# A two-layer mixture-of-experts decoder on one core: shared expert blocks summed by twos, the block order moved, smaller DMA sums, x adds on GpSimd

## The chip, the cores and the metric

The kernel runs on one core of one Trainium2 chip. The metric is the device time of one execution in microseconds (us). Three executions of the kernel before took 2149.96, 2151.9 and 2156.48 us; their median, 2151.9 us, is the time before.

## The reference

Two layers work on x of 512 tokens by 1024 numbers, in float32. Each has a mixer (layer 0: block attention and gated linear attention; layer 1: a gated delta net) and then a mixture of experts (MoE), both closed by a layer norm of `alpha * x + gate * f(...)`. The change lies almost wholly in the MoE:

```python
scores = sigmoid(xf @ router_w)                # 512 x 64 experts
topi   = top 6 of the experts in the 4 best of 8 groups, by scores + bias
topw   = scores[topi] / sum * ROUTED_SCALE
for e in range(64):                            # the tokens that chose e
    routed[tok] += w * ((silu(xf[tok] @ w_gate[e]) * (xf[tok] @ w_up[e])) @ w_down[e])
shared = (silu(xf @ sh_gate) * (xf @ sh_up)) @ sh_down
return routed + shared
```

`w_gate` and `w_up` are 1024 x 256, `w_down` is 256 x 1024: 3 MB of weights per expert, 64 experts, two layers. A layer has 3072 pairs of token and expert.

## The kernel before

The core sorts the experts by their number of tokens (all but the first two) and puts them in 38 blocks of 128 rows per layer: 20 **singles** (one expert each, places 0 to 19 of the sorted list), 14 **twos** (two experts, 64 rows each) and 4 **fours** (32 rows each). `blocks()` builds the table `BLOCKS`; `share()` tells experts with more tokens than their rows to leave the rest to an extra stage that runs only where it is needed.

`moe()` (from L1480 on) goes over the blocks in one loop. For each block there is, on TensorE (PE):

- the **turn** (L1324): 8 transposes of the gathered rows of x;
- **widen** (L1336): the gate and up projections, 16 matmuls;
- the **turn back** (L1347): 2 transposes of the hidden rows;
- **narrow** (L1369): the down projection. A four has 4 weights of 1 MB, and its narrow falls in two halves, each with two of them (the generator yields between).

One turn of the loop issues narrow of block b-1 and widen of block b, the turn of b+1, the turn back of b, and the one-hot matmuls (L1270) that say which tokens block b+2 or b+3 gathers. PE's order is exactly the order in which the Python code issues it (`manual_schedule`); the other engines are ordered by a scheduler.

How the result gets into x differs. A **single** is multiplied on VectorE (DVE, L1375) and added to an array `acc` in DRAM by an indirect DMA of 128 rows that accumulates (L1376, issued by GpSimd, POOL). After the last block, `acc` is read back in 8 pieces (L1615) and added to x by 8 DVE additions (L1616). A **shared** block (two or four) is split into a high and a low part (`yh`, `yl`; L1383 to L1385) and summed by PE with one-hot matrices (**combine**, L1396): for each of 4 token tiles and 2 halves of the columns 2 matmuls fill a bank, and one DVE addition of 128 x 512 (L1397) puts it into x. These 8 rounds per shared block come in two portions of 4: after widen, and after the turn and turn back.

The SP queue loads the weights in order (L1302): gate and up of expert e (2 MB), then down of expert e-3 (1 MB). Gate and up have 5 buffers, down has a ring of 3 (`slot`, L202): a load of down waits until narrow has read the third one before it, a load of gate and up until widen has read the fifth one before it. Whatever stands behind in SP's order waits too.

At the end of layer 0's mixer `out_project` calls `fill`, which works off a queue of small pieces of the modulation of layer 1; its last piece is `mod_end`, 16 transposes (L268) and 4 reductions (L269).

Of the kernel before, what the change touches and what calls it, by code (L numbers as in the profile page):

```python
# [18 lines left out]
P = 128  # L19
# [29 lines left out]

def blocks():  # L50


    def shared(k, n, m):
        w = P // m
        return [tuple((k + (g if j % 2 == 0 else -1 - g) + n * ((j + 1) // 2) // (m // 2), w * j, w)
                      for j in range(m)) for g in range(n // m)]

    def spread(out, more, at0=0.5, end=0):

        n = len(out) + len(more)  # L60
        at = {int((k + at0) * (n - end) / len(more)) for k in range(len(more))}
        a, b = iter(out), iter(more)
        return [next(b if k in at else a) for k in range(n)]

    alone = [((k, 0, P),) for k in range(ALONE)]
    twos = shared(ALONE, TWOS, 2)
    fours = shared(ALONE + TWOS, E - ALONE - TWOS, 4)
    return alone[:SINGLE] + spread(spread(twos, fours), alone[SINGLE:], 0, 1)
# [65 lines left out]
class Kernel:  # L134
# [1032 lines left out]
    def share(self, M):  # L1167
# [4 lines left out]
        runs, k = [], ALONE  # L1172
# [154 lines left out]
    def widen(self, M, G):  # L1327
# [4 lines left out]
        h = G["h"] = M["pool"].tile([P, FE], F32, tag="hh", name="hh", bufs=2)  # L1332
# [18 lines left out]
    def narrow(self, M, G):  # L1351

        nc, hT, pool = self.nc, G["hT"], M["pool"]
        one = G.get("one")
        if one:
            (yh,) = [pool.tile([P, D], FR, tag="yh", name="yh", bufs=2)]
# [14 lines left out]
        if one:  # L1371
            yf = yh.bitcast(F32)
            for h, py in enumerate(pys):
                cs = slice(512 * h, 512 * h + 512)
                nc.vector.tensor_mul(yf[:, cs], py, M["grow"][:, cs])  # L1375
            nc.gpsimd.indirect_dma_start(out=M["acc"], out_offset=bass.IndirectOffsetOnAxis(ap=G["tok"], axis=0),  # L1376
                                         in_=yf, in_offset=None, bounds_check=S + P - 1, compute_op=OP.add)
# [93 lines left out]
    def moe(self, l, hT, nxt, pre=None):  # L1471
# [32 lines left out]
        def loads():  # L1504

            last = []
            for k, b in enumerate(BLOCKS):
# [4 lines left out]
                W.append([(a, n, x) for (_, a, n), x in zip(b, w)])  # L1512
# [40 lines left out]
        with ExitStack() as es:  # L1553
            M["pool"] = self.pool(f"exp{l}", ctx=es)
            todo, units = [], []
# [11 lines left out]
            with self.tc.manual_schedule(engines={mybir.EngineType.PE}):  # L1567
                fetch(sum(2 * len(x) for x in BLOCKS[:LEAD]) + 2)
                self.turn(M, G[0])
                for b in range(NB + 1):  # L1570
# [3 lines left out]
                    if b > 0:  # L1574
                        row.append(self.narrow(M, G[b - 1]))
                        if not G[b - 1]["one"]:
                            todo.append(G[b - 1])
                    if b < NB:
                        fetch(sum(2 * len(x) for x in BLOCKS[:b + LEAD]) + 2)
                        G[b]["w"], G[b]["one"] = W[b], len(W[b]) == 1  # L1580
                        row.append(self.widen(M, G[b]))
                    if not todo:
                        row.reverse()
                    for x in row:
                        next(x)
                    for x in row:
                        for _ in x:
                            pass
                    if todo and b < NB:
                        units = [lambda g=todo, t=t, h=h: self.combine(g, t, h) for t in range(TT) for h in range(2)]  # L1590
                        todo = []
                    for u in units[:4]:
# [3 lines left out]
                    if b < NB and not units:  # L1596
# [3 lines left out]
                    if b < NB and units:  # L1600
# [4 lines left out]
                    units = []  # L1605
# [168 lines left out]
    def run(self):  # L1774
# [5 lines left out]
        with ExitStack() as es:  # L1780
# [8 lines left out]
            def fill(n=3):  # L1789

                n, left[0] = n + left[0], 0
                for i in range(n):
# [5 lines left out]
                    if i and len(queue) == 1:  # L1798
# [12 lines left out]
            self.out_project(mixed, d["ev_w_out"][0], grow, d["x"][0], fill, (0, 1, 4, 5, 6, 7, 2, 3))  # L1811
# [86 lines left out]
```

## Time and profile before

| | |
|---|---|
| median of 3 executions | 2151.9 us |
| profiled execution | 2150.13 us |
| its span in the trace | 2148.1 us |
| mean granted TensorE clock | 0.967 |
| PE busy | 1955.6 us, 91% |
| weight loads of PE (PEld) | 1193.5 us, 56% |
| VectorE busy | 1236.2 us, 58% |
| ScalarE (ACT) busy | 508.3 us, 24% |
| GpSimd busy | 441.2 us, 21% |
| DMA moved | 572.18 MB, mean 266 GB/s |

The span runs from the first to the last instruction of the profiled execution. The expert loop of layer 0 lies at about 402 to 1028 us, that of layer 1 at about 1491 to 2117 us. A granted clock of 1 is 2.4 GHz, 0.5 is 1.2 GHz. The idle time of an engine is put down to what ended it ("releaser").

### The profile page before, as it was taken

How to read it: one execution, taken by the hardware profiler on the slowest of the kernel's cores; microseconds unless marked ns; L12 is line 12 of the kernel's file. 1: busy time of each engine (PE TensorE's matmuls, PEld its weight loads, DVE VectorE, ACT ScalarE, POOL GpSimd, SP SyncE). 2: the span in 40 equal slices, each digit the busy share in tenths (PEclk: the TensorE clock that was granted, in tenths of full speed). 3: DMA queues.
4: the chain of work that ended last, by engine and by line, in shares of the span. 5: the costliest groups of instructions: out<-in, count | busy, mean ns of one | idle time of the engine just before them, and what ended most of it. 6: DMA issues, size and time to landing. Idle time of an engine off the chain costs nothing. (4 is left out here: it accounts for less than half of the span.)

```text
span 2148.1 us, 28655 instructions
## 1 busy us (share of the span) xinstructions
PE 1955.6 (91%) x10619; PEld 1193.5 (56%) x10619; DVE 1236.2 (58%) x3169; ACT 508.3 (24%) x969; POOL 441.2 (21%) x313
## 2 busy tenths in 40 slices
PE   4999878999999999999688999999999999998995
PEld 3777778644443443443567877888443444443432
DVE  6666687844444553542778778578453535544436
ACT  3412533111111111111334455523111111111110
POOL 1222234111010110101034445144211010110102
PEclk9999998999999999999899999999999999999997
DMA  7765455998998989988332111128989989989893
GB/s 296 257 240 186 182 199 195 352 330 325 406 349 351 389 316 361 381 325 300 96 118 59 40 60 60 46 99 309 357 335 365 363 327 402 353 317 405 329 348 126
DMA packets 128679, 572.18 MB, mean 266 GB/s; under 512 B 16943, under 2 KB 54255, under 8 KB 72473
## 3 DMA queue, kind: packets, MB, share of 16 engines
q1 hardware_dynamic: 103600, 499.81, 60.1%
q0 software_dynamic: 19632, 55.79, 9.3%
q10 hardware_dynamic: 5304, 14.72, 1.9%
q8 instruction: 85, 1.39, 0.3%
q14 instruction: 58, 0.47, 0.1%
HBM read 550.33 MB, written 34.61 MB: 272 GB/s over the span
## 5 line engine op out<-in xcount | busy, mean ns | idle before, releaser
L1336 PE MATMUL ps_mm<-wslot,xT 128*64 128x512 f32 (+2 forms) x1216 | 404.5, 596 | 1.1 <-ACT xT L1325 0.8
L1369 PE MATMUL ps_mm<-wslot,hT 128*64 128x512 f32 (+2 forms) x1024 | 329.6, 627 | 20.1 <-DMA wslot<-in_moe_w_down_dram 19.9
L1338 DVE SCALAR_TENSOR_TENSOR hh<-hh,t,ps_mm 128x256 f32<-128x256 f32 x76 | 36.5, 480 | 434.5 <-ACT hh L1337 434.5
L1336 PE MATMUL ps_mm<-parts,xT 128*64 128x512 f32 (+2 forms) x832 | 280.0, 595 | 0.7 <-ACT xT L1325 0.4
L1336 PEld LDWEIGHTS ps_mm<-wslot,xT 128*64 128x64 f32 (+2 forms) x1216 | 142.1, 148 | 218.9 <-issue 205.7
L1369 PEld LDWEIGHTS ps_mm<-wslot,hT 128*64 128x64 f32 (+2 forms) x1024 | 105.5, 152 | 225.1 <-issue 197.5
L232 PE MATMUL ps_mm<-parts,hTh 128*128 128x256 f32 x704 | 206.7, 295 | 14.0 <-DVE op L400 6.9
L1294 POOL DMA_INDIRECT xg<-hd,idx x76 | 86.3, 1136 | 615.1 <-PE ps_tr L1396 525.4
L233 PE MATMUL ps_mm<-parts,hTh 128*128 128x256 f32 x704 | 204.0, 291 | 4.9 <-DVE parts L220 4.2
L234 PE MATMUL ps_mm<-parts,hTl 128*128 128x256 f32 x704 | 203.3, 291 | 0.0
L225 POOL TENSOR_TENSOR parts<-wslot,parts 128x512 fp32r<-128x512 f32 (+1 forms) x79 | 140.6, 1807 | 241.9 <-ACT parts L218 241.8
L1397 DVE TENSOR_TENSOR x<-x,ps_tr 128x512 f32<-128x512 f32 x288 | 183.6, 680 | 11.1 <-PE ps_tr L1396 10.4
L1337 ACT ACTIVATE hh<-ps_mm 128x256 f32<-128x256 f32 x76 | 29.2, 384 | 613.7 <-PE ps_mm L1336 613.7
L1376 POOL DMA_INDIRECT acc<-yh,row x40 | 64.8, 1620 | 498.9 <-DVE yh L1375 498.9
L1336 PEld LDWEIGHTS ps_mm<-parts,xT 128*64 128x64 f32 (+2 forms) x832 | 93.7, 144 | 130.5 <-issue 122.9
L1396 PE MATMUL ps_tr<-yh,ohs 128*128 128x512 f32 x288 | 137.4, 477 | 26.1 <-DVEq L1690 14.0
L232 PEld LDWEIGHTS ps_mm<-parts,hTh 128*128 128x128 f32 x704 | 137.3, 195 | 17.7 <-DVE op L400 4.6
L1325 ACT ACTIVATE xT<-ps_tr 128x512 f32<-128x512 f32 x152 | 84.0, 597 | 245.0 <-PE ps_tr L1324 245.0
L233 PEld LDWEIGHTS ps_mm<-parts,hTh 128*128 128x128 f32 x704 | 137.4, 195 | 6.8 <-DVE parts L220 4.8
L234 PEld LDWEIGHTS ps_mm<-parts,hTl 128*128 128x128 f32 x704 | 136.8, 195 | 2.2 <-issue 0.9
L234 PE MATMUL ps_mm<-hTh,parts 128*128 128x512 f32 (+1 forms) x296 | 120.6, 407 | 9.1 <-POOL parts L225 9.1
L232 PE MATMUL ps_mm<-hTh,parts 128*128 128x512 f32 (+1 forms) x296 | 123.7, 418 | 5.1 <-ACT parts L218 2.5
(456 smaller groups left out, 3124.3 us busy)
## 6 DMA issues: line engine op xcount, KB each, us to landing
wslot<-in_moe_w_down_dram SPq DMA_DIRECT2D x128, 1024.0 KB, 10.4
wslot<-in_moe_w_gate_dram SPq DMA_DIRECT2D x76, 1024.0 KB, 8.2
wslot<-in_moe_w_up_dram SPq DMA_DIRECT2D x76, 1024.0 KB, 11.7
parts<-in_moe_w_gate_dram SPq DMA_DIRECT2D x52, 1024.0 KB, 10.3
parts<-in_moe_w_up_dram SPq DMA_DIRECT2D x52, 1024.0 KB, 8.8
wslot<-in_ada_w_dram SPq DMA_DIRECT2D x44, 1024.0 KB, 5.6
wslot<-in_od_w_in_dram SPq DMA_DIRECT2D x16, 1024.0 KB, 6.2
wslot<-in_ev_w_in_dram SPq DMA_DIRECT2D x12, 1024.0 KB, 6.4
```

Of the source, the lines that this page charges most:

```text
L225: eng.tensor_sub(lo[:, ks], v[:, ks], hi[:, ks].bitcast(F32))
L232: self.nc.tensor.matmul(out, ah, bh, start=(i == 0), stop=False)
L233: self.nc.tensor.matmul(out, ah, bl, start=False, stop=False)
L234: self.nc.tensor.matmul(out, al, bh, start=False, stop=(i == n - 1))
L1294: self.nc.gpsimd.indirect_dma_start(out=xg, out_offset=None, in_=M["hd"], in_offset=bass.IndirectOffsetOnAxis(ap=idx, axis=0), bounds_chec ...
L1325: nc.scalar.activation(xT[:, 4 * g:4 * g + 4], pt.rearrange("p (k c) -> p k c", k=4), AF.Copy)
L1336: nc.tensor.matmul(pv[a:a + n], xT[:, i, a:a + n], w[0][:, :, i], start=(i == 0), stop=(i == KT - 1))
L1338: nc.vector.scalar_tensor_tensor(h, h, G["wt"], pg[:, FE:], op0=OP.mult, op1=OP.mult)
L1369: nc.tensor.matmul(py[a:a + n], hT[:, k, a:a + n], w[1][:, k, 512 * h:512 * h + 512], start=(k == 0), stop=(k == 1))
L1376: nc.gpsimd.indirect_dma_start(out=M["acc"], out_offset=bass.IndirectOffsetOnAxis(ap=G["tok"], axis=0), in_=yf, in_offset=None, bounds_che ...
L1396: nc.tensor.matmul(po, G["oh"][:, t], y[:, cs], start=(i + k == 0), stop=(i == len(Gs) - 1 and k == 1))
L1397: nc.vector.tensor_add(self.x[t][:, cs], self.x[t][:, cs], po)
```

## The change

1. **Combine by twos.** Two shared blocks are collected; then 4 matmuls fill a bank before one DVE addition, 8 rounds for two blocks (`full`, `todo`). Only the last two shared blocks of a layer are summed alone. The number of matmuls stays the same; the additions fall from 18 x 8 to 10 x 8 per layer.
2. **Block order.** `spread(..., 0.5, 3)` turns the row of block sizes from `1 1 1 1 2 1 2 1 4 1 2 1 2 1 2 1 4 ...` into `1 1 1 2 1 2 1 4 1 2 1 2 1 1 2 1 4 ...`; the end turns from `... 4 1 2 2` into `... 1 4 2 2`.
3. **Fours.** The second half of a four's narrow is issued after the turn and turn back, not right behind widen; a pair whose second block is a four is summed one turn of the loop later (`late`).
4. **First of a pair.** Where no sum is due, widen of the single is issued ahead of narrow of the two (`row.reverse()`).
5. **DMA sums.** Singles use a buffer of their own (`ys`, one copy) in place of a copy of `yh`; the buffer `hh` has one copy in place of two. The DMA accumulates only the expert's share of rows: 128 for places 0 to 8, 96 for places 9 to 13, 80 for places 14 to 19. That is 5 x 32 + 6 x 48 = 448 rows of 4 KB less per layer. PE still computes 128 rows.
6. **Reading acc back.** 4 DMAs of 512 KB, in the last three turns of the loop, into the buffers of gathered rows, and 4 additions of 128 x 1024 per layer on GpSimd, in place of 8 DMAs of 256 KB and 8 additions on DVE behind the last turn.
7. **fill.** `out_project` of layer 0 calls `fill(3, False)`, so that `mod_end` comes inside its last stage and not behind it.

```diff
+def width(k):
+    return P if k < SINGLE + 7 else 96 if k < SINGLE + 12 else 80
...
-    alone = [((k, 0, P),) for k in range(ALONE)]
+    alone = [((k, 0, width(k)),) for k in range(ALONE)]
...
-    return alone[:SINGLE] + spread(spread(twos, fours), alone[SINGLE:], 0, 1)
+    return alone[:SINGLE] + spread(spread(twos, fours), alone[SINGLE:], 0.5, 3)
...
-        h = G["h"] = M["pool"].tile([P, FE], F32, tag="hh", name="hh", bufs=2)
+        h = G["h"] = M["pool"].tile([P, FE], F32, tag="hh", name="hh", bufs=1)
...
-            (yh,) = [pool.tile([P, D], FR, tag="yh", name="yh", bufs=2)]
+            yf = pool.tile([P, D], F32, tag="ys", name="ys", bufs=1)
...
-            nc.gpsimd.indirect_dma_start(out=M["acc"], out_offset=bass.IndirectOffsetOnAxis(ap=G["tok"], axis=0),
-                                         in_=yf, in_offset=None, bounds_check=S + P - 1, compute_op=OP.add)
+            nc.gpsimd.indirect_dma_start(out=M["acc"], out_offset=bass.IndirectOffsetOnAxis(ap=G["tok"][:one], axis=0),
+                                         in_=yf[:one], in_offset=None, bounds_check=S + P - 1, compute_op=OP.add)
...
-                    if not todo:
+                    four = b > 0 and len(BLOCKS[b - 1]) > 2
+                    full = len(todo) == 2 or (todo and shared > nshared - 2)
+                    if not full and not four:
                         row.reverse()
                     for x in row:
                         next(x)
-                    for x in row:
+                    for x in row[four:]:
                         for _ in x:
                             pass
-                    if todo and b < NB:
-                        units = [lambda g=todo, t=t, h=h: self.combine(g, t, h) for t in range(TT) for h in range(2)]
+                    units, late = late, []
+                    if full and b < NB:
+                        late = [lambda g=todo, t=t, h=h: self.combine(g, t, h) for t in range(TT) for h in range(2)]
                         todo = []
+                        if not four:
+                            units, late = units + late, []
...
-                    if b == NB - 1:
-                        for t in range(TT):
-                            for h in range(2):
-                                cs = slice(512 * h, 512 * h + 512)
-                                y = self.wk("acc")
-                                nc.gpsimd.dma_start(y, M["acc"][t * P:(t + 1) * P, cs])
-                                nc.vector.tensor_add(self.x[t][:, cs], self.x[t][:, cs], y)
+                    if NB - 3 <= b < NB:
+                        for t in back[b][0]:
+                            nc.gpsimd.tensor_add(self.x[t], self.x[t], M["xg"][(NB - 3 + t) % 3])
+                        for t in back[b][1]:
+                            nc.gpsimd.dma_start(M["xg"][(NB - 3 + t) % 3], M["acc"][t * P:(t + 1) * P])
...
+                    for x in row[:four]:
+                        for _ in x:
+                            pass
...
-                    if i and len(queue) == 1:
+                    if wait and i and len(queue) == 1:
                         left[0] = n - i
                         return
...
-            self.out_project(mixed, d["ev_w_out"][0], grow, d["x"][0], fill, (0, 1, 4, 5, 6, 7, 2, 3))
+            self.out_project(mixed, d["ev_w_out"][0], grow, d["x"][0], lambda: fill(3, False), (0, 1, 4, 5, 6, 7, 2, 3))
```

PE's order at a four, before (the first `hT 32x512` row is the first half of its narrow, the `wslot_4117` row widen of the single behind it, `yh` and `yl` rows are combine):

```order
L1440 MATMUL ps_mm<-wd,sh 128x512 x2
L1369 MATMUL ps_mm<-wslot,hT 32x512 x8
L1336 MATMUL ps_mm<-wslot_4117,xT 128x512 x8
L1369 MATMUL ps_mm<-wslot,hT 32x512 x8
L1396 MATMUL ps_tr<-yh,ohs 128x512
...
L1324 MATMUL ps_tr<-call,xg_2911 128x128 x8
L1347 MATMUL ps_sm<-call,hh 128x128 x2
```

The same place now (lines 1334, 1346, 1357, 1379 and 1449 are the old 1324, 1336, 1347, 1369 and 1440):

```order
L1379 MATMUL ps_mm<-wslot,hT 32x512 x8
L1346 MATMUL ps_mm<-parts,xT 128x512 x8
L1334 MATMUL ps_tr<-call,xg_2910 128x128 x8
L1357 MATMUL ps_sm<-call,hh 128x128 x2
...
L1449 MATMUL ps_mm<-wd,sh 128x512 x2
L1379 MATMUL ps_mm<-wslot,hT 32x512 x8
L1346 MATMUL ps_mm<-wslot_4029,xT 64x512
```

The turn, the turn back and a piece of the shared expert (L1449) now stand between widen and the second half, and no combine stands between the second half and widen of the next two (the `64x512` row).

PE's order at the two that follows a four, behind widen of that two and narrow of the single, before:

```order
L1369 MATMUL ps_mm<-wslot,hT 128x512 x4
L1347 MATMUL ps_sm<-call,hh 128x128 x2
L1324 MATMUL ps_tr<-call,xg_2912 128x128 x8
...
L1440 MATMUL ps_mm<-wd,sh 128x512 x2
L1369 MATMUL ps_mm<-wslot,hT 64x512 x8
L1336 MATMUL ps_mm<-parts,xT 128x512 x8
L1396 MATMUL ps_tr<-yh,ohs 128x512
L1396 MATMUL ps_tr<-yl,ohs 128x512
```

Now:

```order
L1379 MATMUL ps_mm<-wslot,hT 128x512 x4
L1357 MATMUL ps_sm<-call,hh 128x128 x2
L1334 MATMUL ps_tr<-call,xg_2911 128x128 x8
...
L1379 MATMUL ps_mm<-wslot,hT 64x512 x8
L1346 MATMUL ps_mm<-wslot_4117,xT 128x512 x8
L1405 MATMUL ps_tr<-yh,ohs 128x512
L1405 MATMUL ps_tr<-yl,ohs 128x512
```

Narrow of the two keeps its place behind the single; behind it, and behind widen of the next single, comes the sum of a pair (L1405), 16 matmuls there and 16 after the turn.

The end of a layer, now (the last four, then the two twos; the second `hT 64x512` row reads a weight from another buffer):

```order
L1346 MATMUL ps_mm<-wslot_16179,xT 64x512
L1334 MATMUL ps_tr<-call,xg_11979 128x128 x8
L1357 MATMUL ps_sm<-call,hh 128x128 x2
L1379 MATMUL ps_mm<-wslot,hT 32x512 x8
L1379 MATMUL ps_mm<-wslot,hT 64x512
L1379 MATMUL ps_mm<-wslot_16270,hT 64x512
```

Narrow of the first of the two twos follows the second half of the four at once; before, a single stood between the last four and these twos.

## Rows read from the trace of the kernel before

**Rows 1.** Page: busy times, DMA queues (packets, MB, share of 16 engines).

```profile
PE 1955.6 (91%) x10619; PEld 1193.5 (56%) x10619; DVE 1236.2 (58%) x3169; ACT 508.3 (24%) x969; POOL 441.2 (21%) x313
...
q0 software_dynamic: 19632, 55.79, 9.3%
```

**Rows 2.** Windows: length; busy PE, PEld, DVE, ACT, POOL; clock, DMA share, GB/s.

```profile
400.00:1000.00 600.00, 577.31 (x2380) 260.29 (x2379) 277.98 (x847) 79.01 (x150) 68.12 (x55) 0.98 0.93 356
500.00:600.00 100.00, 96.57 (x409) 42.88 (x410) 45.18 (x135) 12.11 (x23) 9.94 (x8) 1.00 0.97 376
...
980.00:990.00 10.00, 7.03 (x15) 1.47 (x15) 1.23 (x2) 0.63 (x1) 0.00 (x0) 0.66 1.01 428
```

**Rows 3.** Waits of PE: total us, times, longest us.

```profile
PE ps_mm L1369 <- DMA wslot<-in_moe_w_down_dram: 19.9, 8, 4.2
PE ps_tr L1396 <- DVEq L1690: 14.0, 2, 8.0
...
PE ps_tr L1396 <- DVE yl L1385: 7.8, 9, 1.0
```

**Rows 4.** Timeline of PE, sum of one two: start us, duration us, instruction, [idle].

```profile
579.51 0.80 PE L1396 MATMUL ps_tr<-yh,ohs 128*128 128x512 f32 x1
...
580.38 0.40 PE L1396 MATMUL ps_tr<-yh,ohs 128*128 128x512 f32 x1
580.62 0.39 PE L1396 MATMUL ps_tr<-yl,ohs 128*128 128x512 f32 x1
...
582.26 1.31 PE L1324 MATMUL ps_tr<-call,xg 128*128 128x128 f32 x8
...
583.75 0.48 PE L1396 MATMUL ps_tr<-yh,ohs 128*128 128x512 f32 x1
...
585.89 0.64 PE L1336 MATMUL ps_mm<-parts,xT 128*64 128x512 f32 x1
```

**Rows 5.** Timeline of PE: second half of a four's narrow, first and last four.

```profile
544.88 3.62 PE L1369 MATMUL ps_mm<-wslot,hT 128*32 128x512 f32 x14 [1.40 <-DMA wslot<-in_moe_w_down_dram]
...
982.81 6.61 PE L1369 MATMUL ps_mm<-wslot,hT 128*32 128x512 f32 x14 [3.01 <-DMA wslot<-in_moe_w_down_dram]
```

**Rows 6.** PE and SP behind the first four; landing of that load, of all.

```profile
548.43 0.50 PE L1396 MATMUL ps_tr<-yh,ohs 128*128 128x512 f32 x1
...
555.58 7.09 PE L1336 MATMUL ps_mm<-wslot,xT 128*64 128x512 f32 x32
...
569.36 3.65 PE L1369 MATMUL ps_mm<-wslot,hT 128*64 128x512 f32 x16
...
547.69 0.33 SPq L1302 DMA_DIRECT2D wslot<-in_moe_w_down_dram  x1
...
wslot<-in_moe_w_down_dram SPq DMA_DIRECT2D x1, 1024.0 KB, 13.4
...
DMA to landing us min/median/max: 4.6/10.0/20.6
```

**Rows 7.** Timeline of SP: loads behind narrow of a two.

```profile
573.04 0.33 SPq L1302 DMA_DIRECT2D wslot<-in_moe_w_down_dram  x1
...
581.15 0.33 SPq L1302 DMA_DIRECT2D wslot<-in_moe_w_down_dram  x1
```

**Rows 8.** Timeline at the end of each layer, and a GpSimd operation of 128 x 1024.

```profile
1018.85 0.50 PE L1396 MATMUL ps_tr<-yh,ohs 128*128 128x512 f32 x1
...
1036.01 0.79 PE L1396 MATMUL ps_tr<-yh,ohs 128*128 128x512 f32 x1 [7.98 <-DVEq L1690]
...
2108.36 0.50 PE L1396 MATMUL ps_tr<-yh,ohs 128*128 128x512 f32 x1
...
2123.06 0.79 PE L1396 MATMUL ps_tr<-yh,ohs 128*128 128x512 f32 x1 [6.01 <-DVEq L1690]
...
2129.88 2.38 POOL L330 TENSOR_TENSOR x<-x,wd 128x1024 f32<-128x1024 f32 x1 [1.55 <-ACT x L329]
```

**Rows 9.** Timeline of PE ahead of the MoE of layer 0.

```profile
355.39 1.12 PE L268 MATMUL ps_tr<-call,acc 128*128 128x128 f32 x4 [4.12 <-DVE mod L269]
```

More of the change, by code (lines that the diff above doesn't have):

```diff
@@ L1171, in share @@
         of = {k: (a, n) for b in BLOCKS for k, a, n in b}
-        runs, k = [], ALONE
+        runs, k = [], SINGLE
+        for n in sorted({width(k) for k in range(SINGLE, ALONE)}, reverse=True):
+            m = sum(width(j) == n for j in range(SINGLE, ALONE))
+            if n < P:
+                runs.append((k, k + m))
+            k += m
         for n, m in ((TWOS, 2), (E - ALONE - TWOS, 4)):
@@ L1353, in narrow @@
         nc, hT, pool = self.nc, G["hT"], M["pool"]
-        one = G.get("one")
+        one = G.get("one", 0)
         if one:
-            (yh,) = [pool.tile([P, D], FR, tag="yh", name="yh", bufs=2)]
+            yf = pool.tile([P, D], F32, tag="ys", name="ys", bufs=1)
         elif "y" not in G:
@@ L1371, in narrow @@
         if one:
-            yf = yh.bitcast(F32)
             for h, py in enumerate(pys):
@@ L1511, in loads @@
                 w = [[] for _ in es]
-                W.append([(a, n, x) for (_, a, n), x in zip(b, w)])
+                W.append([(a, n if len(b) > 1 else P, x) for (_, a, n), x in zip(b, w)])
                 for x, e in zip(w, es):
@@ L1554, in moe @@
             M["pool"] = self.pool(f"exp{l}", ctx=es)
-            todo, units = [], []
+            todo, late, shared = [], [], 0
+            nshared = sum(len(b) > 1 for b in BLOCKS)
+            back = {NB - 3: ((), (0, 1)), NB - 2: ((0, 1), (2, 3)), NB - 1: ((2, 3), ())}
             for _ in range(NXG - SINGLE):
@@ L1577, in moe @@
                             todo.append(G[b - 1])
+                            shared += 1
                     if b < NB:
                         fetch(sum(2 * len(x) for x in BLOCKS[:b + LEAD]) + 2)
-                        G[b]["w"], G[b]["one"] = W[b], len(W[b]) == 1
+                        G[b]["w"], G[b]["one"] = W[b], len(W[b]) == 1 and BLOCKS[b][0][2]
                         row.append(self.widen(M, G[b]))
-                    if not todo:
+                    four = b > 0 and len(BLOCKS[b - 1]) > 2
+                    full = len(todo) == 2 or (todo and shared > nshared - 2)
+                    if not full and not four:
                         row.reverse()
@@ L1595, in moe @@
                         ahead()
-                    if b < NB and not units:
+                    if b < NB and not units and not four:
                         self.turn_back(M, G[b])
@@ L1599, in moe @@
                         self.turn(M, G[b + 1])
-                    if b < NB and units:
+                    if b < NB and (units or four):
                         self.turn_back(M, G[b])
@@ L1604, in moe @@
                         u()
-                    units = []
                     if b == NB - 3 and pre:
@@ L1787, in run, with fill @@
             left = [0]
-            def fill(n=3):
+            def fill(n=3, wait=True):
                 n, left[0] = n + left[0], 0
```

## The prediction

> **What bounds the kernel now.** First the page and the stretches. PE is busy for 1955.6 of 2148.1 us, VectorE for 58% of them [rows 1]; in the loop of layer 0, from 400 to 1000 us, PE is busy for 577.31 of 600 us at a clock of 0.98, and at the same time the DMA engines are busy for 93% of it and move 356 GB/s [rows 2]. Two things stand close together there: PE has 22.7 us left, the transfers have 7%, some 42 us. So I take PE's own work for the bound, and the moment a weight lands for what lies next below. Then PE's waits: in the whole kernel 19.9 us for weights of the down projection in 8 places, 7.8 us for `yl`, 14.0 us in two places at the layers' ends [rows 3]. Then the timelines, which show what PE does where the change cuts in.
>
> **How a sum of one two runs.** Its 8 matmuls from 579.51 hold PE until the turn at 582.26, 2.75 us; the other 8, from 583.75, until widen at 585.89, 2.14 us [rows 4]. Two matmuls of a full sequence start 0.24 us apart (580.38, 580.62), so 16 of them would need 3.8 us and not 4.89: every second matmul waits for a free bank, that is for an addition on VectorE.
>
> **Part by part**, both layers together, against the 2150.1 us of the profiled execution.
>
> *A, sums by twos.* A pair costs 2 x 4.89 = 9.8 us now. With four matmuls to a bank VectorE has half the additions, and 32 matmuls at 0.24 us take 7.7 us. 8 pairs per layer: 16 x 2.1 = **-34 us**. The two last blocks of a layer are summed as before. The 128 additions that go per two layers are on VectorE, which is not the bound, and count for nothing else.
>
> *B, `yl`.* PE begins a sum right behind the narrow that makes it and waits for VectorE and ScalarE. Now a widen, or the whole rest of the turn of the loop, stands between: **-7.6 us** of 7.8 [rows 3].
>
> *C, second halves of fours.* All 8 waits for a down weight are there: each four, each layer. One wait of 1.40 us is followed by 14 matmuls in 3.62 us, one of 3.01 us by the same in 6.61 [rows 5]; in the ten microseconds of the second the granted clock is 0.66 [rows 2], a mean of the levels 1.2 and 2.4 GHz, after a pause of PE. The mean of the 8 waits is 2.5 us, the longest 4.2; I take the longer half of them to cost 3.0 us more each. The second half now has the turn and the turn back ahead of it, 1.5 us, and in half of the places a piece of the shared expert too, 1.9 us. I leave 5 of the 19.9 us and 2 of the 12 us of slow clock: **-25 us**. Bounds: nothing gone, if the weights come later by as much; all 32 us gone.
>
> *D, the wait that takes its place.* The ring of the down weights has three buffers. The two that follows the first four gets its weights only as the four's second half releases them; the first one is issued at 547.69 and takes 13.4 us, where half of all weights take up to 10.0 and the longest 20.6 [rows 6]; the queue is full there, as the four has let go four pairs of gate and up at once. It lands at 561.1. Behind it in SP's order stand 2 MB of gate and up and then the second one, 3 MB; at 0.42 MB per microsecond (I take it between the 376 GB/s of 100 us and the 428 of ten, nearer to the latter as the queue is full [rows 2]), that is 7.5 us, so it lands at about 568.6, and narrow reads it at 569.36 [rows 6], 0.7 us later. Of the 20.9 us between the end of the second half (548.43) and narrow (569.36), the sum of the four is 7.15 (548.43 to 555.58) [rows 6]. The change takes this sum away from there, and nothing else comes in: widen, narrow of the single and the turn, 13.8 us, are all that is left. So narrow comes 7.15 us earlier, the weight at most 0.5 us (the DMA sum in the queue is shorter): wait 7.15 - 0.7 - 0.5 = 6 us, and 3 us of slow clock behind it by the longer of rows 5. This holds for the first and the second four of each layer, whose two is the second of its pair: 4 x 9 = 36 us. Behind the third four a widen of 7 us stands ahead of narrow, and it is covered. Behind the last four the two stands without any single: from the end of the first half there are widen of that two (7.1 us), the turns (1.5) and the second half (3.6), 12.2 us, and in that time SP sends four more megabytes and one ahead of them, 5 MB, which at the same pace take 12.5 us, with 2 us until the last lands (the shortest landing of 1 MB is 4.6). That is 2.5 us with an empty queue and 6 with one load ahead: I take 5.5 and 3 of clock, 2 x 8.5 = 17. Together **+53 us**; bounds 20 (queue empty, no slow clock) and 75.
>
> *E, ends of the layers.* From the end of the last widen to the first of the last sums it is 17.2 us in layer 0 (1018.85 to 1036.01) and 14.7 in layer 1 (2108.36 to 2123.06), of which PE idles 7.98 and 6.01 [rows 8]; VectorE is there busy with 8 additions of `acc`. Now: the pair's 7.7 us stand there, a stop of about 2.4 us (the next block's `yh` waits until the pair has been read), 3.8 for that block's own sums, 0.3 turn back, 3.65 narrow, and 0.5 until the sums begin: 18.3. Less the 7.7 which A has counted: 10.6, against 17.2 and 14.7: **-10 us**. The additions of `acc` go to GpSimd, which takes 2.38 us for one operation of that size [rows 8]: 4 per layer, 9.5 us; two of them lie beside widen and the sums. If they lie on the path, the 10 us are 5.
>
> *F, `fill`.* PE stands 4.12 us for the reductions between the transposes of `mod_end` [rows 9], behind the last matmuls of the mixer. Inside the last stage they have matmuls beside them: **-5 us**, bounds 0 and -10.
>
> *G.* One buffer `hh`, one `ys`: a single's sum must have left the buffer before the next single's product. They lie 13 us or more apart, but for a few neighbours 12; the issue is hidden or costs VectorE some microseconds that PE does not see. Six more small operations in `share`, each layer: **+1 us**. The 896 rows less are 3.67 MB; at the pace of their queue (55.79 MB in 9.3% of the span, 200 us [rows 1]) 13 us of the engines' time, which lies beside PE's work.
>
> Sum: -34 - 7.6 - 25 + 53 - 10 - 5 + 1 = -27.6, so 2122.5 us for an execution like the profiled one. The median of the three is 1.8 us above it: **2124 us**, 1.3% less.
>
> **The rivals.**
>
> *R1, slower: the ring of three is late at every second two.* In a pair of twos, narrow of the second now comes about 13.6 us behind narrow of the first; up to now two portions of sums and a widen lay between as well, 11 us. If its weights then wait as in D, that is four more places per layer: 8 x 9 = 72 us, 2196 us. The change is slower than before from 28/8 = 3.5 us per place on. For it: the 10.0 us of the middle landing and the tail up to 20.6 [rows 6]. Against it: now the second of the two loads is issued at 581.15, 8 us behind the first (573.04), since gate and up between them wait for the widen that comes after narrow [rows 7]; with widen ahead of narrow, both go out within 1.5 us. That leaves 12 us for 4 MB, some 10 us at 0.42 MB per microsecond, where no four has filled the queue. Chance 0.08.
>
> *R2, no new waits:* the weights behind a four come as much earlier as narrow does, because the wait of the second half itself (which holds back their issue) is gone. Then D falls away: 2124 - 53 = 2071 us. Against it: gate and up loads ahead in the same queue set the landing, not the issue. Chance 0.10.
>
> *R3, transfers set the pace of the loops.* Then PE's savings in A to C turn into waits, and only E, F and the bytes count: 3.67 MB at 356 GB/s are 10 us, with E and F 25 us: 2127 us. For it: 0.93 and 356 GB/s over 600 us. Against it: over 100 us the rows show 0.97 and 376, over ten even 428 GB/s [rows 2], so there is room for the 15 us that my loops shrink by (2.4% of 356 is 365 GB/s). Chance 0.12. By the Trainium skill (DMA: Bandwidth & Descriptors, Specifications) the HBM gives one core some 358 GB/s, and by this rule the loops, at 356, could not get shorter but by bytes, so it speaks for R3. The rows at 376 to 428 GB/s do not agree with it as a ceiling for this run.
>
> *R4, no difference:* the second halves of fours stay late, as their weights hang on the same ring, and C gives 5 and not 25 us, D stands: 2144 us. Chance 0.13. That the narrower DMA sums send experts to the extra stage is no case: by the reference's inputs the fullest expert of the 96-row places has 81 tokens, that of the 80-row places 72.
>
> **How the numbers follow.** The forecast has 0.57, with its own range from the bounds of C, D and E: 2098 to 2142. A measurement of this kernel tells 0.3%, 6.5 us, from no change: faster means under 2145.4. Faster: forecast 0.54, R2 0.10, R3 0.11, R4 0.06, in all 0.81. Same: 0.03 + 0.01 + 0.07 = 0.11. Slower: R1's 0.08. The range from 2088 to 2145 leaves out R1, R2 and a little at each end.
>
> **What would show it.** A: the additions on VectorE behind the sums fall from 288 to 160, and PE's pairs take 7.7 us. B: the wait for `yl` is below 1 us. C: waits for down weights in the second halves below 2 us each. D: new waits of 4 to 8 us at the twos behind the first, second and last four, with a clock near 0.7 behind them. E: PE idles under 3 us at the last sums. Wrong would be: waits at the second two of other pairs (R1), none behind the fours (R2), or a DMA share of the loops still at 0.93 with waits spread over many blocks (R3).

## The result, and the profile after

The change took 2177.24 us (median of 4 executions, 2170.82 to 2180.92), the kernel before 2150.93 on the same chips (4 executions, 2146.26 to 2156.48): ratio 1.0118, interval 1.0083 to 1.0154. It is **slower by 26 us**; the prediction had 28 us less, and its range ends at 2145. The profiled execution took 2180.92 us, its span is 2179.0, the mean granted clock 0.951 where it had been 0.967.

The page of the change, its rows for busy times, the DMA queue of GpSimd and the sums of shared blocks (matmuls L1405, additions L1406):

```profile
PE 1958.1 (90%) x10619; PEld 1222.5 (56%) x10619; DVE 1167.3 (54%) x3037; ACT 504.4 (23%) x969; POOL 459.6 (21%) x313
...
q0 software_dynamic: 18608, 52.12, 8.1%
...
L1405 PE MATMUL ps_tr<-yh,ohs 128*128 128x512 f32 x288 | 127.9, 445 | 21.0 <-DVE x L1406 10.9
...
L1406 DVE TENSOR_TENSOR x<-x,ps_tr 128x512 f32<-128x512 f32 x160 | 108.1, 686 | 31.1 <-PE ps_tr L1405 29.2
```

The additions fell to 160, the bytes by 3.67 MB [rows 1], VectorE is less busy: the change does what part 1 and part 5 say. The waits of PE (total us, times, longest), against [rows 3]:

```profile
PE ps_mm L1379 <- DMA wslot<-in_moe_w_down_dram: 55.3, 13, 9.3
PE ps_mm L237 <- ACT hTh L356: 11.6, 4, 5.4
...
PE ps_tr L1405 <- DVE x L1406: 10.9, 9, 3.8
...
PE ps_tr L1405 <- DVEq L1708: 9.9, 2, 5.0
```

The wait for `yl` has gone from among them; that for down weights has grown by 35 us. Its places, in PE's timeline: the first four and the two behind it, then the last four and the first of the last twos:

```profile
535.51 4.68 PE L1379 MATMUL ps_mm<-wslot,hT 128*32 128x512 f32 x16
...
553.45 1.04 PE L1379 MATMUL ps_mm<-wslot,hT 128*64 128x512 f32 x2 [1.41 <-DMA wslot<-in_moe_w_down_dram]
563.82 5.83 PE L1379 MATMUL ps_mm<-wslot,hT 128*64 128x512 f32 x14 [9.33 <-DMA wslot<-in_moe_w_down_dram]
...
995.74 3.62 PE L1379 MATMUL ps_mm<-wslot,hT 128*32 128x512 f32 x14 [0.67 <-DMA wslot<-in_moe_w_down_dram]
1005.84 1.94 PE L1379 MATMUL ps_mm<-wslot,hT 128*64 128x512 f32 x2 [6.47 <-DMA wslot<-in_moe_w_down_dram]
1008.58 4.89 PE L1379 MATMUL ps_mm<-wslot,hT 128*64 128x512 f32 x13 [0.80 <-DMA wslot<-in_moe_w_down_dram]
```

These are the places of step D, and the waits are longer than its 6 and 5.5 us: 10.7 and 7.3. The 14 matmuls behind the long wait take 5.83 us. Over both layers 51.2 us of the 55.3 stand at the twos behind fours and 4.1 at the second halves of the fours, the longest of those 1.65 us.

Now the stretch from the sum ahead of the four to the end of its second half, in the change and in the kernel before; then its end alone and the stretch behind the long wait, both in the change (columns as in [rows 2]):

```profile
500.00:541.00 41.00, 40.88 (x186) 16.97 (x186) 14.92 (x57) 4.70 (x10) 4.65 (x4) 1.00 0.85 326
```

```profile
508.00:549.00 41.00, 39.33 (x169) 14.87 (x168) 14.00 (x44) 3.61 (x7) 3.68 (x3) 1.00 0.92 352
```

```profile
525.00:541.00 16.00, 15.88 (x56) 6.40 (x56) 4.35 (x16) 2.14 (x5) 0.99 (x1) 1.00 1.02 381
...
560.00:570.00 10.00, 6.18 (x15) 1.85 (x16) 1.70 (x3) 0.63 (x1) 0.00 (x0) 0.59 1.01 408
```

SP's loads there, in the change:

```profile
528.54 0.33 SPq L1312 DMA_DIRECT2D parts<-in_moe_w_up_dram  x1
539.38 0.33 SPq L1312 DMA_DIRECT2D wslot<-in_moe_w_down_dram  x1
540.22 0.33 SPq L1312 DMA_DIRECT2D parts<-in_moe_w_gate_dram  x1
...
541.32 0.33 SPq L1312 DMA_DIRECT2D wslot<-in_moe_w_down_dram  x1
```

SP stands from 528.9 to 539.4, 10.5 us: the next down load waits until the second half has read its weights, and everything behind it in SP's order waits too. That alone is not new: before, SP stood for 8.5 us at the same place, up to 547.69 [rows 6]. Nor do the DMA engines run dry meanwhile: from 525 to 541 us they are busy all the time, with loads that are out already. The lower rate of the whole stretch, 326 for 352 GB/s, comes from ahead of it, and it alone does not make the wait either (`f2_fours` below has 327 and waits 2.87 us).

What is new is that narrow comes sooner. From the issue of the two's first weight to its narrow there were 21.7 us (547.69 to 569.36); now there are 12.7 (539.38 to 552.04, where the first wait begins). I call this time the **cover** of the loads. The second weight, issued at 541.32, is there at 563.8, 22.5 us behind its issue, beyond the longest landing of before [rows 6].

The ends of the layers: PE's first sum behind the last widen, and the first of the last sums, in layer 0 and in layer 1; then VectorE and GpSimd in between in layer 0:

```profile
1020.70 0.50 PE L1405 MATMUL ps_tr<-yh,ohs 128*128 128x512 f32 x1
...
1045.57 0.80 PE L1405 MATMUL ps_tr<-yh,ohs 128*128 128x512 f32 x1 [4.94 <-DVEq L1708]
...
2130.09 0.50 PE L1405 MATMUL ps_tr<-yh,ohs 128*128 128x512 f32 x1
...
2152.76 0.79 PE L1405 MATMUL ps_tr<-yh,ohs 128*128 128x512 f32 x1 [4.95 <-DVEq L1708]
```

```profile
1031.10 3.28 DVE L1406 TENSOR_TENSOR x<-x,ps_tr 128x512 f32<-128x512 f32 x5
...
1037.96 3.94 DVE L1396 TENSOR_SCALAR ohs<-call,t 128x128 fp32r<-128x128 f32 x3
1041.82 0.68 DVE L1392 TENSOR_TENSOR y<-ps_mm,grow 128x512 f32<-128x512 f32 x1
...
1036.94 4.67 POOL L1629 TENSOR_TENSOR x<-x,xg 128x1024 f32<-128x1024 f32 x2 [30.24 <-DVE x L1406]
```

24.9 and 22.7 us, where I had 18.3, against 17.2 and 14.7 [rows 8]. GpSimd's last two additions wait for the sums and then run beside the last block's one-hots on VectorE (the matrices that PE needs for its sums): three of these take 3.94 us, which took 0.68 nine microseconds earlier (at 1029.10). PE idles 4.94 us between the last narrow and its sums.

### The profile page after: what moved, and what is told of

Read it like the earlier page. It is cut to its first block, busy times and chain, and to the rows that moved or that the text cites. A ratio compares the mean times of both kernels' runs of the same rounds, so it can differ in the third digit from the quotient of the medians.

```text
span 2179.0 us, 28504 instructions
## 1 busy us (share of the span) xinstructions
PE 1958.1 (90%) x10619; PEld 1222.5 (56%) x10619; DVE 1167.3 (54%) x3037; ACT 504.4 (23%) x969; POOL 459.6 (21%) x313
## 5 line engine op out<-in xcount | busy, mean ns | idle before, releaser
L1346 PE MATMUL ps_mm<-wslot,xT 128*64 128x512 f32 (+2 forms) x1216 | 410.5, 605 | 3.5 <-ACT xT L1335 2.6
L1379 PE MATMUL ps_mm<-wslot,hT 128*64 128x512 f32 (+2 forms) x1024 | 334.1, 625 | 55.5 <-DMA wslot<-in_moe_w_down_dram 55.3
L1346 PE MATMUL ps_mm<-parts,xT 128*64 128x512 f32 (+2 forms) x832 | 301.3, 603 | 1.1 <-ACT xT L1335 0.9
L1304 POOL DMA_INDIRECT xg<-hd,idx x76 | 93.0, 1224 | 526.7 <-PE ps_tr L1405 211.0
L1346 PEld LDWEIGHTS ps_mm<-parts,xT 128*64 128x64 f32 (+2 forms) x832 | 102.5, 148 | 131.3 <-issue 121.3
L1385 POOL DMA_INDIRECT acc<-ys,row x40 | 61.6, 1541 | 537.5 <-DVE ys L1384 537.5
L1405 PE MATMUL ps_tr<-yh,ohs 128*128 128x512 f32 x288 | 127.9, 445 | 21.0 <-DVE x L1406 10.9
L1406 DVE TENSOR_TENSOR x<-x,ps_tr 128x512 f32<-128x512 f32 x160 | 108.1, 686 | 31.1 <-PE ps_tr L1405 29.2
## 6 DMA issues: line engine op xcount, KB each, us to landing
wslot<-in_moe_w_up_dram SPq DMA_DIRECT2D x76, 1024.0 KB, 12.3
```

What stands on the lines that cost most here:

```text
L1304: self.nc.gpsimd.indirect_dma_start(out=xg, out_offset=None, in_=M["hd"], in_offset=bass.IndirectOffsetOnAxis(ap=idx, axis=0), bounds_chec ...
L1346: nc.tensor.matmul(pv[a:a + n], xT[:, i, a:a + n], w[0][:, :, i], start=(i == 0), stop=(i == KT - 1))
L1379: nc.tensor.matmul(py[a:a + n], hT[:, k, a:a + n], w[1][:, k, 512 * h:512 * h + 512], start=(k == 0), stop=(k == 1))
L1405: nc.tensor.matmul(po, G["oh"][:, t], y[:, cs], start=(i + k == 0), stop=(i == len(Gs) - 1 and k == 1))
L1406: nc.vector.tensor_add(self.x[t][:, cs], self.x[t][:, cs], po)
```

## The experiments

Each time is a median of 4 to 10 executions; the kernel before gave 2150.1 to 2153.0 in the same jobs, so differences to the change, which ran in a job of its own, hold to some 3 us. Times within a layer are those of one profiled execution per run.

**The waits behind the fours, and at the last twos.** `e1_behind` issues widen of the next single ahead of narrow of the two behind a four, and the pair's sum one turn of the loop later:

```diff
+behind = full and b > 2 and len(BLOCKS[b - 3]) > 2 and not four
-if not full and not four:
+if (not full and not four) or behind:
     row.reverse()
...
-    if not four:
+    if not four and not behind:
         units, late = units + late, []
```

> The change, but in the turn of the loop that has narrow of the two behind the first and second four, widen of the next single is issued ahead of that narrow, and the pair's sum one turn later. Theory (the down weights of that two come late since the ring of three lets them go only behind the four): widen gives 6.6 to 7 us of cover, the waits of 9.3 and some 7 us per layer fall below 3 us each and the slow clock behind them (3 us each) goes: about 19 us per layer less, 2177 - 38 = about 2139 us. Rival (transfers set the pace of the loop, the wait only stands where the slack is smallest): the waits turn up at later narrows, the time stays above 2165 us.

2139.96 us, 37 less than the change, ratio to before 0.9953 (0.9937 to 0.9969), as the theory had it. The cover behind the first four is 20.0 us again (533.77 to 553.72). Waits for down weights:

```profile
PE ps_mm L1379 <- DMA wslot<-in_moe_w_down_dram: 25.9, 12, 6.5
```

`e2_last` has `or b == NB - 1` in that condition and nothing else of it:

> The change, but widen of the last two is issued ahead of narrow of the first of the two last twos. Theory (that narrow waits for its own weights, 6.5 + 0.8 us in layer 0 and slow clock behind): 7 us of cover, 8 to 10 us per layer less, 2158 to 2161 us. Rival (the time is lost again at the last sums, which wait for VectorE anyway): within 5 us of 2177.

2156.11 us, 21 less, somewhat more than the theory's 16 to 19; the wait fell from 55.3 to 39.8 (in the longest of the ten executions, 2171.41 us: it was the profiled one). So D stood where it was put, and the two repairs, each alone, are worth 37 and 21 us, 58 in the sum. The rival in which transfers set the pace falls for these two places: no wait of that size turned up elsewhere.

**GpSimd's additions, and fill.** `e3_dve_add`: `nc.vector.tensor_add` for `nc.gpsimd.tensor_add`.

> The change, but the 4 additions of acc to x per layer are on VectorE in the same places, not on GpSimd. Theory (GpSimd's 128 x 1024 additions hold VectorE up while they run, and two of them run just where VectorE makes the last block's one-hots): the three one-hot operations that take 3.94 us take 0.7, VectorE gets 2 additions of 1.3 us there in exchange; 0 to 3 us per layer less, 2171 to 2177 us. Rival (the two engines do not hinder each other): the one-hots still take 3.9 us and the end of each layer gets longer by 2.6 us, 2182 us.

2170.80 us, 6 less, at the theory's edge. The ends of the layers (from the first sum behind the last widen to the last sums) take 22.2 and 20.0 us there, 2.7 and 2.6 less. In its VectorE timeline the one-hots are short again, and an addition that waits for its DMA holds the queue up:

```profile
1000.21 1.23 DVE L1629 TENSOR_TENSOR x<-x,xg 128x1024 f32<-128x1024 f32 x1 [18.72 <-DMA xg<-acc]
...
1031.34 0.68 DVE L1396 TENSOR_SCALAR ohs<-call,t 128x128 fp32r<-128x128 f32 x3 [0.22 <-PE ps_tr L1405]
```

PE's turn back waits 12.3 us for VectorE there (at 1005.65). In layer 0 that covers the wait for the last twos' weights, which ends at 1005.84 in the change.

`e4_no_fill`: `out_project(..., fill, ...)` again.

> The change without its part on fill: mod_end comes behind the last stage of out_project again. Theory (its transposes only moved 2 us of PE work into the stage, and the wait behind it, 5.37 us for ScalarE's copy, is that of the norm on VectorE): 0 to 3 us less, 2174 to 2177, and the first widen at 402.5 and not 403.7. Rival (my forecast: the change gained 5 us there): 5 us more, 2182.

2173.02 us (2170.0 to 2176.24): the ranges overlap, so no gain of fill is shown, and 5 us more is excluded.

**Both moves, with the additions of acc placed otherwise.** `c1_early` issues GpSimd's additions ahead of the sums; `c2_hybrid` has `eng = nc.gpsimd if t < 2 else nc.vector`.

> The change with both moves of narrow (behind the first and second four; the last two), and with the additions of acc on GpSimd issued ahead of a turn's sums and not behind them. Theory (the waits for down weights are the loss, each stands at its own place, and GpSimd's additions hold VectorE up where the last one-hots are made): 2140 - 21 for the last two - 3 to 4 us per layer at the ends, 2109 to 2119 us. Rival (once the largest waits are gone the transfers set the pace): the two moves do not add up, above 2125 us, with waits at other narrows.

> The change with both moves of narrow, and with the first two additions of acc per layer on GpSimd, the last two on VectorE in their place behind the sums. Theory: the last one-hots no longer run beside GpSimd, 3.3 us less, two additions of 1.3 us more on VectorE: 2140 - 21 - 0 to 3 us per layer, 2113 to 2119 us, that is at or a few us above the run with all four on GpSimd but earlier. Rival (VectorE is the bound of the layer's end whatever stands there): both runs give the same end of the layer, within 1 us.

2126.57 and 2120.04 us, 51 and 57 less than the change. c1 misses its theory and stands where its rival was put, above 2125; but the rival's waits are not there: those for down weights are 12.5 us in the sum. So the moves do not add up fully, and why is open. c2 comes out 6.5 us shorter than c1, where its theory had it no shorter. Part of it lies at the ends: 25.6 and 20.7 us in c1, 21.3 and 20.0 in c2, 4.9 less in the sum. That fits that GpSimd beside VectorE costs more than two more additions on VectorE.

**Step A alone.** `a1_banks`, on e1_behind: in `combine` each block of the pair has its own bank and addition.

> The change with the move behind the first and second four (measured 2140 us), but each shared block of a pair has its own bank and its own addition again: the order of PE's matmuls by banks is 2 and 2, not 4, and the additions on VectorE are 288 again. Theory (step A: two matmuls per addition wait for VectorE, four do not): 16 pairs by 2.1 to 2.6 us more, 2174 to 2182 us. Rival (PE's slack at the weights swallows it: what the sums lose, the waits for weights give back): less than half of it, below 2157 us.

2190.08 us, 50 more than e1_behind. The two portions of a pair's sum, each from its first matmul to the next instruction, there and in the change:

```profile
584.03 0.80 PE L1405 MATMUL ps_tr<-yh,ohs 128*128 128x512 f32 x1
...
589.47 1.31 PE L1334 MATMUL ps_tr<-call,xg 128*128 128x128 f32 x8 [0.18 <-DVE x L1406]
...
590.96 0.47 PE L1405 MATMUL ps_tr<-yh,ohs 128*128 128x512 f32 x1
...
596.10 4.45 PE L1346 MATMUL ps_mm<-wslot,xT 128*128 128x512 f32 x10
```

```profile
576.15 0.80 PE L1405 MATMUL ps_tr<-yh,ohs 128*128 128x512 f32 x1
...
580.21 1.05 PE L1334 MATMUL ps_tr<-call,xg 128*128 128x128 f32 x8
...
581.54 0.47 PE L1405 MATMUL ps_tr<-yh,ohs 128*128 128x512 f32 x1
...
585.28 1.88 PE L1449 MATMUL ps_mm<-wd,sh 128*128 128x512 f32 x4
```

5.44 + 5.14 us against 4.06 + 3.74: 2.8 a pair, and the ends are 7 us longer in the sum than in e1_behind. So A is real. But a1's pair is also longer than two sums of the kernel before (9.8 us by the prediction's rows). Against those, 7.80 us save 2.0 a pair, 32 us for 16 pairs, which is what A had; the 50 us are what the shared bank is worth in this arrangement.

**DMA sums alone.** `s1_sums` is the kernel before with `width`, `ys`, `hh` of one copy and the rows `[:one]`; `s2_rows` is c2_hybrid with `width` always 128.

> The kernel before with part 5 alone: DMA sums of 96 or 80 rows for the less full experts, a buffer of their own, one buffer hh. Theory (PE is the bound of the loops, the 13 us of DMA time lie beside it): 0 to 4 us less, by shorter waits at the fours, 2147 to 2151 us. Rival (transfers set the pace): 10 to 13 us less, 2137 to 2141 us.

> The same version (2120 us), but the DMA sums have 128 rows again for all singles. Theory from the run with part 5 alone (19 us less: the down weights land about a microsecond earlier, and the waits fall under the length behind which the clock falls): 12 to 20 us more, 2132 to 2140 us. Rival (my step G: nothing on the path): 0 to 4 us more.

2131.63 us, 19 less than before, beyond both theories; 2126.17, 6 more than c2_hybrid, between theory and rival. s1_sums has the fewer rows and the other buffers together; s2_rows takes back the rows alone. What the buffers do in the kernel before was not run apart. The waits of s1_sums and their longest:

```profile
PE ps_mm L1379 <- DMA wslot<-in_moe_w_down_dram: 15.4, 9, 3.0
```

They are 4.5 us less than before, the mean clock is 0.973 and not 0.967: at the third four the wait of 3.54 us with 14 matmuls in 6.41 became 2.67 us with 3.62. Before, three of the eight fours have such slow matmuls, in all 7.5 us beyond 3.62 each; in s1_sums none has. So waits and slow matmuls make 12 of the 19 us, and the rest is open.

**Second halves of fours.** `f1_fours` (on c2_hybrid) and `f2_fours` (on the change): `for x in row:` for `for x in row[four:]:`.

> The version with both moves of narrow and the mixed additions of acc (2120 us), but the second half of a four's narrow stands right behind widen again (part 3 undone). Theory (step C: the second half waits for its weights, and a long wait is followed by slow clock): waits for down weights up by 1.5 us or more in each of 8 places and slow clock at two to four of them, 18 to 25 us more, 2138 to 2145 us. Rival (with the smaller DMA sums the weights land early enough, or the turns only change places with the wait): 0 to 8 us more, below 2128 us.

> The change as it was timed (2177 us), but the second half of a four's narrow stands right behind widen again (part 3 undone). Theory now (the later second half lets the ring of down buffers go later, so what it gains at itself it gives away at the two that follows): the waits at second halves grow by some 10 us in the sum, those at the twos behind fours shrink by 2 to 3 us each, with less slow clock: 2168 to 2178 us. Rival (my step C, 25 us with slow clock): 2190 to 2200 us.

2121.61 us, 1.6 more; 2174.66 us (2170.91 to 2175.69), 2.6 less, both with overlapping ranges: no gain of 25 us in either. In f2_fours the second half waits again and the two behind it less; then the waits of f2_fours in all, and SP's stand:

```profile
536.44 5.32 PE L1379 MATMUL ps_mm<-wslot,hT 128*32 128x512 f32 x14 [3.17 <-DMA wslot<-in_moe_w_down_dram]
...
560.71 5.34 PE L1379 MATMUL ps_mm<-wslot,hT 128*64 128x512 f32 x14 [2.87 <-DMA wslot<-in_moe_w_down_dram]
```

```profile
PE ps_mm L1379 <- DMA wslot<-in_moe_w_down_dram: 47.2, 15, 6.0
```

```profile
528.58 0.33 SPq L1312 DMA_DIRECT2D parts<-in_moe_w_up_dram  x1
540.75 0.33 SPq L1312 DMA_DIRECT2D wslot<-in_moe_w_down_dram  x1
```

Of these 47.2 us 17.9 stand at second halves and 29.3 at the twos behind, where the change has 4.1 and 51.2. SP stands longer than in the change, 11.8 us. The cover is what differs: 16.1 us (540.75 to 556.80, narrow's first matmul) for 12.7. The turn, the turn back and the piece of the shared expert, 3.2 us, stand behind the second half here and ahead of it in the change.

**acc, and route_extra.** `g1_read` (on c2_hybrid) reads acc as the kernel before; `c3_route` (on c2_hybrid) has `if b == 2: self.route_extra(M)` for `b == 4`, and fill as before.

> The same version (2120 us), but acc is read back as in the kernel before: 8 DMAs and 8 additions on VectorE behind the last turn (part 6 undone). Theory of my step E: 5 to 10 us more, 2125 to 2130 us. Rival, as the trace of the change has it (the layer's end hangs on VectorE's chain of additions, split and one-hots, and part 6 gives nothing there): within 3 us of 2120.

> The same version (2120 us), with route_extra two turns of the loop earlier, where a single and no two has just been computed, and fill as before the change. Theory (PE waits there twice for VectorE, 2.16 and 1.81 us, since the split of the first two stands in VectorE's queue, and the next widen runs at slow clock, 9.83 for 7.09 us): 3 to 6 us per layer less, 2108 to 2114 us. Rival (the wait is route_extra's own chain and moves with it): 2117 to 2121 us.

g1_read: 2123.29 us (2119.44 to 2129.14), 3 more than c2_hybrid (2119.07 to 2122.12): the ranges overlap, so no difference is shown. In the profiled executions the ends are 26.0 and 25.1 us without part 6, 4.8 and 5.0 more than with it, but the way from the first widen to the end of the last one is shorter by 8.0 and 3.4.

c3_route: 2114.92 us, 5 less (2105.1 to 2117.46): nearer the theory, just outside its range. It undoes part 7 as well, so the 5 us are not those of route_extra alone.

**The row of blocks.** `o1_order`: `spread(..., 0, 1)`; it leaves out the last single's rows in the first two token tiles. `o2_order_read` has the reading of acc of before too and leaves out nothing.

> The change with the row of blocks of the kernel before (part 2 undone), all else as it is. Theory (the last two twos have a single ahead of them again, so the wait there, 7 us and slow clock behind it, does not arise; the twos behind the first and second four stay late): as much as moving the last widen gave, 17 to 22 us less, 2155 to 2160 us. Rival (the order of blocks is not the cause at the end; any pair there waits): within 6 us of 2177.

> The change with the row of blocks and the reading back of acc of the kernel before (parts 2 and 6 undone). In the run with the row alone, o1_order, the first reads of acc stand ahead of the last single's DMA sum, so that its rows were left out of the first two token tiles; here nothing is left out. Theory (the row of blocks costs the change what o1_order gained, 46 us, and part 6 is worth 0 to 5 us): 2131 to 2138 us. Rival (o1_order was short because it read acc too early): above 2145 us.

2131.36 and 2132.10 us: 46 and 45 less, twice what moving the last widen gave and far more than the theory had. The end of layer 0 in o1_order:

```profile
1007.56 0.50 PE L1405 MATMUL ps_tr<-yh,ohs 128*128 128x512 f32 x1
...
1021.48 1.19 PE L1405 MATMUL ps_tr<-yh,ohs 128*128 128x512 f32 x2 [4.67 <-DVEq L1708]
```

13.9 us against 24.9. With the old row the last four's pair is summed one single earlier, and the wait at the last twos does not arise. By the profiled executions the two ends are 22 us shorter, the two loops up to the last widen 26.

**Both causes repaired.** `c5_best` is o2_order_read with `behind`; `c6_best` reads acc in 4 DMAs in the last two turns and adds 128 x 1024 on VectorE.

> As o2_order_read, and widen of the single ahead of narrow of the two behind the first and second four, the pair's sum one turn later. Theory (the waits there are separate from those of the row of blocks, so the two repairs add): 37 us less than o2_order_read, 2095 to 2101 us. Rival (transfers set the pace below some 2115 us): 10 to 20 us less.

> As c5_best, but acc is read back in 4 DMAs in the last two turns and added by 4 additions of 128 x 1024 on VectorE. Theory (the additions stand on VectorE's chain at the layer's end either way, 8 of 0.6 us or 4 of 1.3 us; only their wait for the DMAs goes): 0 to 4 us less than c5_best. Rival (an addition that waits for its DMA holds VectorE's queue up, as in e3_dve_add, where the turn back waited 12.3 us): more than c5_best by 3 us or more.

2108.10 and 2106.87 us; c6_best stands at 0.9801 of the kernel before (0.9779 to 0.9823), 70 us under the change. `behind` gave 24 us here and not 37, between theory and rival. In the old row it takes hold at a third place too: a four stands three blocks ahead of the last two, so widen of the last two comes ahead of narrow of the first. From the last four to the next layer, and in layer 1 to the end, c5_best takes 1.8 and 3.5 us longer than o2_order_read by their profiles. The waits of c6_best for down weights:

```profile
PE ps_mm L1379 <- DMA wslot<-in_moe_w_down_dram: 8.8, 9, 2.3
```

## Why the prediction was wrong

The mechanism that I gave the largest price, D, is there, at its places and near its size: 53 forecast, 58 recovered by two moves. That the size came out is in part luck: 35 us of it were waits, where 51 were measured, and of these C's move makes 22 (29.3 without it). The sign turned on other steps.

- **C (-25) failed.** The second halves do wait less, 4.1 us in all where they had 19.9, but the change does not gain by it: undone, it is 2.6 us faster, which the ranges don't tell from no difference. The step that failed is the overlap: the turn, the turn back and the piece of the shared expert, which C puts ahead of the second half, had stood behind it, where they were cover for the next narrow. Against f2_fours the second halves save 13.8 us of waits and the twos behind pay 21.9 (at the first four 9.33 us with the move, 2.87 without). I counted C and D as two terms; the same work can cover only one of the two waits. D has it wrong by itself too: its 13.8 us between second half and narrow hold that piece of the shared expert; measured were 11.9 (540.12 to 552.04). R2 spoke of the link: the loads do go out sooner than without the move, by 1.4 us, but narrow comes 4.8 us sooner (552.04 for 556.80). R4 had C at 5 us, for second halves that stay late; they do not.
- **E (-10) failed.** The ends are 7.7 and 8.0 us longer, which is just the pair's sum that A already counts, so E came to 0. The term that was mis-sized is the 0.5 us from the last narrow to the sums: it is 4.94 and 4.95, which makes 4.4 of the 6.6 us by which the first end exceeds my 18.3, and all of the 4.4 of the second. VectorE's one-hots and splits stand one behind the other there, and GpSimd's last additions hold them up by 3.3 us; I had taken these additions for work beside the path. With them on VectorE (e3_dve_add) the ends are 2.7 and 2.6 us shorter.
- **The row of blocks was not priced** but for 17 us in D at the last twos. It costs 45: 21 for that wait by e2_last, the rest mostly at the ends, where the old row has 13.9 us in layer 0 and the new one 24.9. At route_extra, too, a split of a two now stands ahead in VectorE's queue. PE waits twice, where it waited once before (2.28 us at 464.67), and the next widen runs slowly (9.83 for 7.09 us; before, a narrow did, 5.78 for 3.65):

```profile
467.28 0.21 PE L1241 MATMUL ps_sm<-supper_b,rx 64*64 64x64 bf16 x1 [2.16 <-DVE rx L1238]
...
469.34 1.11 PE L1254 MATMUL ps_sm<-call,rx 64*128 64x64 f32 x4 [1.81 <-DVE rx L1251]
```

- **F (-5) failed:** the wait of 4.12 us [rows 9] became one of 5.37 for ScalarE's copy (at 358.22), which stands in its queue behind the issue of a DMA that needs a norm from VectorE. I took the wait for its last releaser and did not ask what was late next.
- **A (-34) and B (-7.6) held.** A pair takes 7.80 us (7.7 forecast). My reading of [rows 4] was too broad, though: not every second matmul waits for VectorE there, the matmuls from 580.38 on follow each other at 0.24 us, and only the fourth round of a portion comes late. The wait for `yl` went from 7.8 to 0.4 us; what that is worth in time was not run. **G was mis-sized** the other way: part 5, set at +1, is worth 19 us in the kernel before, and its rows alone 6 in the repaired one.

Of the 53 us between 2124 and 2177, C, E and F make 40 by these runs, the row of blocks beyond D's 17 another 28, and part 5 takes some back. The terms overlap (E and the row of blocks share the ends, C and D the cover), and I can't divide them more finely. R1, the slower case, is not what happened: its places, the second twos of other pairs, show no such waits. R3's test does not decide by its share: from 400 to 1000 us it is 0.92 at 351 GB/s, little under the 0.93 and 356 of before [rows 2]. But the waits are not spread over many blocks, as R3 would have them; they stand at the fours and the twos behind them, and go when these are moved. And c6_best moves more:

```profile
400.00:960.00 560.00, 546.81 (x2317) 264.04 (x2317) 232.04 (x750) 74.63 (x147) 73.14 (x54) 0.99 0.95 367
```

The Trainium skill's figure for one core (DMA: Bandwidth & Descriptors, Specifications, some 358 GB/s) is no ceiling here: these 367 GB/s stand above it, and so do the 408 behind the long wait. With 5% of the DMA engines' time left, the transfers may well be what lies next; no run shows it.

## What to carry to other kernels

Two narrows that hang on one small ring and one in-order queue can't be costed apart: work that is moved ahead of the first to cover its wait is gone as cover ahead of the second. Count, for every load, the time from the moment its buffer comes free to the moment it is read. Ask of a new order of blocks what it does at the last blocks and at one-off stages, not only in the steady pattern. Work given to another engine is free only where it doesn't run beside its neighbour's short operations.

## What the runs showed of the hardware

GpSimd's additions of 128 x 1024 held VectorE up: three one-hots of 128 x 128 took 3.94 us beside two of them and 0.68 without, and in e3_dve_add, with the additions on VectorE, no such slow group stands there. The first one-hot, from 1037.96, took 1.43 us and ended at 1039.39, the next ended at 1041.70; GpSimd's additions ended at 1039.30 and 1041.61, 0.09 us ahead of each. The Trainium skill (SBUF — State Buffer, SBUF: two separate sides) says that VectorE and GpSimd share a pair of ports, and that one of the two holds it for a whole instruction when VectorE's operation needs it; the trace agrees with it in these ends.

Waits of PE can cost more than their length: behind the 9.33 us the 14 matmuls took 5.83 us, and the clock of those ten microseconds was 0.59, between the levels of 1.2 and 2.4 GHz; behind waits of 1.40 [rows 5] and 2.67 us they took 3.62. The length of the wait alone does not tell which: in s2_rows the 14 matmuls behind 2.37 us (at 850.08) took 5.32, in s1_sums those behind 3.03 us (at 1924.25) took 3.62. At the third four of s1_sums a wait that was 0.87 us shorter went with 3.7 us saved; this is one place, and no rule.
